# A decoder trunk whose FFN up projections become 2x2x2 block products in seven steps

## The chip, the cores and the metric

The kernel runs on one core of a Trainium2 chip. The metric is the device time of one execution in microseconds; the median of several runs counts.

## The reference, cut to what matters

Two layers work on a residual stream x of 1024 tokens and 1024 channels. Each ends in a convolutional FFN, with D_FF = 2816 and a causal convolution of width 3 over the tokens:

```python
def conv_ffn(h, w_up, w_dw, b_dw, w_down):
    u = h @ w_up                       # [1024, 1024] @ [1024, 5632]
    u = causal_dwconv(u, w_dw, b_dw)
    gate, val = jnp.split(u, 2, axis=-1)
    return (jax.nn.silu(gate) * val) @ w_down

x = x + conv_ffn(rmsnorm(x, g_ffn[l]), w_up[l], w_dw_f[l], b_dw_f[l], w_down[l])
```

Around it stand, in layer 0, a Conformer convolution module with a memory attention beside it and an output projection; in layer 1, a forgetting attention with a memory attention and an output projection. All is float32.

## The kernel before

Channels lie on partitions, tokens along the free axis, in two halves of 512 tokens (`HS`). x is eight tiles `x[k]` of 128 channels by 1024 tokens (tag `x`, eight buffers). A float32 operand is split in two parts that TensorE takes exactly: `split` (lines 77 to 85) makes hi on ScalarE by a cast (line 81) and lo = source - hi (line 82), on GpSimd where nothing else is named. `mm3` (line 103) then makes three matmuls for each k tile: hi hi, hi lo and lo hi.

`ffn` (line 336) first calls `normed` (line 174), which multiplies x by the gain of the norm and splits it (lines 168 and 169), and forms 1/rms of each token as a row `rb` on all partitions; the projection runs on the unscaled values and `rb` is multiplied into its result. `up(c)` handles the hidden tile c of 22: for the gate half and the value half (s = 0, 1) it loads a 1024 x 128 block of w_up, splits it, and makes for both token halves 8 k tiles x 3 matmuls of 512 columns, 96 in all, into a PSUM tile `u` of two banks. VectorE multiplies u by rb in PSUM (line 368), ScalarE applies the tap of the same token and the bias (Identity, line 371), VectorE adds the two earlier tokens from PSUM (lines 373 and 375), ScalarE applies Silu to the gate, VectorE multiplies gate and value (line 384), and the product g is split (tiles gh and gl). A block of w_down is loaded and split too.

Up and down alternate: with G = 2, after two new tiles c the down projection of the two tiles before is made. `down_part` (line 389) accumulates its tiles in one PSUM bank and VectorE adds that to x (line 393). In layer 1 the last two tiles go through `down_final`, 256 tokens at a time, with the last norm.

The order on each engine is worked out when the kernel is built, from the order in the text as priority and from modelled times. DMAs go through the queue of SyncE (SP). Raw weights have two buffers (`raw`), the split ones three (`wh`, `wl`), the w_down ones three of their own. PSUM has eight banks: `c0` to `c3`, used in a ring, and two pairs `b2a` and `b2b`.

Before the first FFN stands the output projection of layer 0 (`out_part`, line 328, called for both halves and m = 0 to 7), whose addition at line 334 finishes x[m].

Of the kernel before, what the change touches and what calls it, by code (L numbers as in the profile page):

```python
# [36 lines left out]
# columns of the packed per-channel vectors: name -> (number of columns)  # L37
# [14 lines left out]
class Trunk:  # L52
# [24 lines left out]
    def split(self, hi, lo, src, lo_eng=None, scale=None):  # L77
        """hi = float32r(src * scale); lo = src * scale - hi, both exact to 24 bits together."""
# [8 lines left out]
    def load_w(self, src, shape, gains=None, name="w", pools=None, lo_eng=None):  # L87
        """DMA one weight unit and split it; shape is the free shape of the unit."""
# [14 lines left out]
    def mm3(self, out, terms, start=True, stop=True):  # L103
        """out (+)= sum over terms of (ah + al)^T (bh + bl) without al^T bl (below 2^-24)."""
# [8 lines left out]
    # The projections run on x * gain; the factor 1/rms of a token is applied to their results  # L113
    # (in layer A to x before the split).
# [3 lines left out]
    def bcast_row(self, col, nb, tag="b1"):  # tag: of a new PSUM tile, or the place itself  # L118
        """col [128 tokens, nb] -> PSUM [128, nb*128] holding col as a row on every partition."""
# [7 lines left out]
    def rstd_cols(self, acc, nb, n, eps, ps=None):  # L127
        """acc [128 ch, nb*128 tokens] partial sums of squares -> 1/sqrt(mean + eps) [128 tokens, nb]."""
# [16 lines left out]
    def sum_squares(self, xs, w=HS, eng=None, tmp=None, two=None):  # L145
        """sum of the squares of xs; from index two on, a second sum on VectorE, added at the end."""
# [48 lines left out]
    def mem_k(self, mh, ml, rb, ks, wk):  # L195
        """K of the memory (stacked hi/hi and lo/lo), scaled."""
# [15 lines left out]
    def mem_v(self, mh, ml, rc, vs, wv):  # L212
        """V of the memory (hi | lo)."""
# [121 lines left out]

    def ffn(self, l):
        nc, tc = self.nc, self.tc
        with tc.tile_pool(name=f"ffn{l}", bufs=1) as fp:
            hh, hl, rb, _ = self.normed(f"f{l}", f"g_ffn{l}")
            gs = {}  # L340

# [968 lines left out]
```

## Time and profile before

| | |
|---|---|
| median of 3 runs | 2437.65 us (2437.09 to 2443.01) |
| span of the profiled execution, its first to its last instruction | 2435.7 us |
| whole time of the profiled execution | the profile gives only its span; the median of the runs is 1.95 us longer |
| TensorE busy | 2360.1 us, 97% |
| VectorE, ScalarE, GpSimd busy | 54%, 39%, 40% |
| mean granted TensorE clock | 0.988 |
| DMA | 156.93 MB, 64 GB/s in the mean |

The first FFN lasts from about 427 to 1146 us, the second from about 1692 us to the end. A row of a group of instructions gives the line of the kernel, the engine, the operation, output and inputs, and its count and durations. PE is TensorE, PEld its weight loads, DVE is VectorE, ACT is ScalarE, POOL is GpSimd and SP is SyncE. In a row of a stage stand its bounds and length, then for each engine the busy time and the count, then the granted clock, the busy share of the DMA engines and GB/s. In a row of the timeline stand start, length, engine, line and operation; `x2` means two of them in one row.

### The profile page before, as it was taken

What the parts mean: (1) busy time and instruction counts of PE and PEld (TensorE: products, weight loads), DVE (VectorE), ACT (ScalarE), POOL (GpSimd) and SP (SyncE); (2) the same over time, 40 slices, a digit from 0 to 9 for tenths busy, and PEclk for the clock granted to TensorE, in tenths of its full rate; (3) what the DMA queues carried; (4) which work ended last, traced back from release to release, by engine and by line L of the source; (5) the groups of instructions that cost most, each with busy time, mean ns of one, the idle gap of its engine ahead of it and who ended that gap; (6) DMA issues with size and microseconds to landing.
All of it is one profiled execution on the core that took longest, in us unless ns stands there. A gap on an engine that the chain in (4) does not pass through costs nothing.

```text
span 2435.7 us, 29247 instructions
## 1 busy us (share of the span) xinstructions
PE 2360.1 (97%) x11450; PEld 1964.7 (81%) x11450; DVE 1319.6 (54%) x1807; ACT 947.3 (39%) x1544; POOL 963.8 (40%) x643
## 2 busy tenths in 40 slices
PE   6999899999999999999998999999999999999998
PEld 6777678888888888887897888778888888888887
DVE  7489774444444444446646777854444444444436
ACT  6786655422222222223543665744322222222222
POOL 3686838422232323333423444525323222322223
PEclk9999989999999999999999999999999999999999
DMA  6110113211111111111432222331111111111112
GB/s 232 35 35 27 62 39 99 78 52 44 53 37 51 44 52 52 52 52 52 149 104 76 72 78 75 113 108 61 61 52 47 49 52 44 51 37 52 44 35 70
DMA packets 64537, 156.93 MB, mean 64 GB/s; under 512 B 6704, under 2 KB 26928, under 8 KB 64400
## 3 DMA queue, kind: packets, MB, share of 16 engines
q1 hardware_dynamic: 64256, 154.75, 20.4%
q8 instruction: 90, 1.47, 0.3%
q14 instruction: 47, 0.39, 0.0%
q10 hardware_dynamic: 144, 0.32, 0.0%
HBM read 128.63 MB, written 20.12 MB: 61 GB/s over the span
## 4 chain that ended last, share of the span: by engine, by line
PE 86%; DVE 6%; POOL 3%; ACT 2%; issue 2%; DMA 0%; DVEq 0%; POOLq 0%; ACTq 0%
PE u L108 13%; PE u L110 13%; PE u L109 13%; PE dn L108 6%; PE dn L110 6%; PE dn L109 6%; PE vps L850 3%; PE pq L108 2%; PE pq L110 2%; PE pq L109 2%; PE op L110 2%; PE op L109 2%; PE op L108 2%; PE fo L1033 1%; PE ft L1024 1%
## 5 line engine op out<-in xcount | busy, mean ns | idle before, releaser
L393 DVE TENSOR_TENSOR x<-x,dn 128x512 f32<-128x512 f32 (+1 forms) x368 | 241.1, 663 | 223.9 <-PE dn L110 221.0
L368 DVE TENSOR_TENSOR u<-u,rb 128x1024 f32<-128x1024 f32 x88 | 108.5, 1233 | 454.2 <-PE u L110 454.2
L82 POOL TENSOR_TENSOR wu_lo<-wu_raw,wu_hi 128x1024 fp32r<-128x1024 f32 x88 | 212.5, 2415 | 351.8 <-ACT wu_hi L81 351.8
L108 PE MATMUL dn<-gh,wd_hi 128*128 128x512 f32 (+1 forms) x736 | 282.1, 383 | 2.7 <-DVE x L393 2.5
L110 PE MATMUL dn<-gh,wd_lo 128*128 128x512 f32 (+1 forms) x736 | 279.7, 381 | 0.3 <-POOL wd_lo L82 0.3
L109 PE MATMUL dn<-gl,wd_hi 128*128 128x512 f32 (+1 forms) x736 | 279.9, 380 | 0.0
L108 PE MATMUL u<-f1h,wu_hi 128*128 128x512 f32 x704 | 274.5, 390 | 0.0
L108 PE MATMUL u<-f0h,wu_hi 128*128 128x512 f32 x704 | 274.5, 390 | 0.0
L109 PE MATMUL u<-f0l,wu_hi 128*128 128x512 f32 x704 | 274.4, 390 | 0.0
L110 PE MATMUL u<-f1h,wu_lo 128*128 128x512 f32 x704 | 274.3, 390 | 0.0
L109 PE MATMUL u<-f1l,wu_hi 128*128 128x512 f32 x704 | 274.3, 390 | 0.0
L110 PE MATMUL u<-f0h,wu_lo 128*128 128x512 f32 x704 | 274.2, 390 | 0.0
L82 POOL TENSOR_TENSOR wd_lo<-wd_raw,wd_hi 128x1024 fp32r<-128x1024 f32 x44 | 107.0, 2432 | 416.0 <-ACT wd_hi L81 416.0
L81 ACT CAST wd_hi<-wd_raw 128x1024 fp32r<-128x1024 f32 x44 | 46.2, 1050 | 449.2 <-PE dn L109 329.6
L82 POOL TENSOR_TENSOR gl<-y,gh 128x512 fp32r<-128x512 f32 x88 | 111.7, 1291 | 208.0 <-ACT gh L81 208.0
L81 ACT CAST wu_hi<-wu_raw 128x1024 fp32r<-128x1024 f32 x88 | 92.4, 1050 | 250.9 <-PE u L109 233.5
L373 DVE SCALAR_TENSOR_TENSOR y<-u,vecs,y 128x1023 f32<-128x1023 f32 x88 | 112.9, 1283 | 110.8 <-ACT y L371 110.8
L108 PEld LDWEIGHTS dn<-gh,wd_hi 128*128 128x128 f32 x736 | 138.3, 188 | 32.2 <-DVE x L393 5.0
L110 PEld LDWEIGHTS dn<-gh,wd_lo 128*128 128x128 f32 x736 | 138.1, 188 | 28.4 <-POOL wd_lo L82 0.5
L109 PEld LDWEIGHTS dn<-gl,wd_hi 128*128 128x128 f32 x736 | 138.5, 188 | 27.4
L108 PEld LDWEIGHTS u<-f1h,wu_hi 128*128 128x128 f32 x704 | 132.1, 188 | 28.0 <-issue 0.3
L108 PEld LDWEIGHTS u<-f0h,wu_hi 128*128 128x128 f32 x704 | 132.1, 188 | 28.0 <-issue 0.3
(349 smaller groups left out, 5399.3 us busy)
## 6 DMA issues: line engine op xcount, KB each, us to landing
wu_raw<-in_wup SPq DMA_DIRECT2D x88, 512.0 KB
wd_raw<-in_wdn SPq DMA_DIRECT2D x44, 512.0 KB
wia_raw<-in_wia SPq DMA_DIRECT2D x14, 512.0 KB
wo_raw<-in_wout SPq DMA_DIRECT2D x16, 384.0 KB
d_v<-vo SPq DMA_DIRECT2D x24, 256.0 KB
vsf<-d_v SPq DMA_DIRECT2D x12, 512.0 KB
x<-in_xT SPq DMA_DIRECT2D x16, 256.0 KB
x<-in_xT SPq DMA_DIRECT2D x8, 512.0 KB
```

The lines of the kernel that those rows point to most:

```text
L81: nc.scalar.copy(hi, src)
L82: (lo_eng or nc.gpsimd).tensor_tensor(lo, src, hi.bitcast(F32), op=ALU.subtract)
L108: nc.tensor.matmul(out, lhsT=ah, rhs=bh, start=start and i == 0, stop=False)
L109: nc.tensor.matmul(out, lhsT=ah, rhs=bl, start=False, stop=False)
L110: nc.tensor.matmul(out, lhsT=al, rhs=bh, start=False, stop=stop and i == n - 1)
L368: nc.vector.tensor_tensor(u, u, rb, op=ALU.mult)
L373: nc.vector.scalar_tensor_tensor(y[:, 1:], u[:, :S - 1], self.vec(wd, FW * j + 1), y[:, 1:], op0=ALU.mult, op1=ALU.add)
L393: return nc.vector.tensor_tensor(self.x[m][:, sl], self.x[m][:, sl], ps, op=ALU.add)
L850: nc.tensor.matmul(ps, lhsT=a[hf][k][:, tsl], rhs=w[:, k % 4], start=k == 0 and j == 0, stop=k == KD - 1 and j == 2)
L1024: mm = nc.tensor.transpose(pt[:, u, P:], p1[:, j * P:(j + 1) * P], self.ident)
L1033: nc.tensor.matmul(po, lhsT=vs[:, j], rhs=pl[:, u], start=False, stop=j == 2 * I + 1)
```

## The change

The two blocks of w_up of one c and the two halves of the input channels form a 2x2 block matrix A: A11 and A12 are the gate's rows for k tiles 0 to 3 and 4 to 7, A21 and A22 those of the value. B has the two halves of the channels (rows) by the two halves of the tokens (columns). Their product takes seven block products instead of eight (Winograd's form): of the left operands A11, A12, A22 and four sums S1 to S4, and of the right ones B11, B21, B22 and four sums T1 to T4.

- `ffn_operands` makes the right operands once for each FFN. x goes to DRAM (`d_x`) first, then its tiles are overwritten with the sums. T1 to T4 need both token halves.
- In `sums`, GpSimd makes S1 to S4 for each c, and `left` splits each of the seven left operands (128 x 512), two to a buffer of `wh` and `wl`; a fourth buffer is added.
- `p1` to `p7` are the products, 4 k tiles x 3 matmuls of 512 columns each, 84 for each c, in three PSUM banks. Between products that share a bank, ScalarE or VectorE reads the partial sum out; VectorE's additions combine them in SBUF tiles g and v (tag `x`). Product 4 of tile c comes after product 1 of tile c + 1.
- `conv` does what it did, but reads g and v in SBUF; the product goes to a DRAM tensor `d_g`.
- When all 22 tiles are done, x comes back from `d_x`, and the down projection runs over groups of 2, 4, 4, 4, 4 and 4 tiles; `prep` loads w_down and g and splits them, the low part of g on VectorE. The last four go through `down_final` in layer 1.
- The output projection of layer 0 takes m in the order 0, 4, 1, 5, 2, 6, 3, 7.

Comments and docstrings are dropped, which changes no instruction. The core of the diff, with the removed lines left out:

```diff
+    def chain(self, out, a, b, start):
+        nc = self.nc
+        ah, al = a
+        bh, bl = b
+        n = len(bh)
+        for k in range(n):
+            for j, (w, h) in enumerate(((ah, bh), (ah, bl), (al, bh))):
+                mm = nc.tensor.matmul(out, lhsT=w[:, k], rhs=h[k], start=start and k == 0 and j == 0,
+                                      stop=k == n - 1 and j == 2, skip_group_check=True)
+        return mm
+    def ffn_operands(self, l, fp):
+        nc = self.nc
+        K2 = KD // 2
+        gain = f"g_ffn{l}"
+        x = self.x
+        h0, h1 = slice(0, HS), slice(HS, S)
+        names = ("B11", "B21", "B22", "T1", "T2", "T3", "T4")
+        ops = {n: ([None] * K2, [None] * K2) for n in names}
+        def op(n, k):
+            for i in range(2):
+                if n in ("T1", "T2", "T3"):
+                    t = fp.tile([P, HS], F32R, tag="h2", name=f"f{n}{i}{k}", bufs=6 * K2)
+                else:
+                    t = self.htile(f"f{n}{i}{k}")
+                ops[n][i][k] = t
+            return ops[n][0][k], ops[n][1][k]
+        for k in range(KD):
+            for hf, sl in enumerate((h0, h1)):
+                nc.sync.dma_start(self.d_x[:, k, sl], x[k][:, sl])
+        for n, o in (("B11", 0), ("B21", K2)):
+            for k in range(K2):
+                self.split_gain(*op(n, k), x[k + o][:, h0], self.vec(gain, k + o))
+        rb = self.main.tile([P, S], F32, tag="rb", name="rb")
+        def stats(hf):
+            sl = (h0, h1)[hf]
+            acc = self.sum_squares([x[k][:, sl] for k in range(KD)], two=5 if hf else None)
+            def rest():
+                r = self.rstd_cols(acc, 4, D, self.eps_rms)
+                nc.scalar.copy(rb[:, sl], self.bcast_row(r, 4))
+            return rest
+        rests = [stats(0), stats(1)]
+        for k in range(K2):
+            g, g2 = self.vec(gain, k), self.vec(gain, k + K2)
+            x11, x12, x21, x22 = x[k][:, h0], x[k][:, h1], x[k + K2][:, h0], x[k + K2][:, h1]
+            nc.scalar.activation(x11, x11, AF.Copy, scale=g)
+            nc.vector.scalar_tensor_tensor(x12, x12, g, x11, op0=ALU.mult, op1=ALU.subtract)
+            self.split_gain(*op("B22", k), x22, g2)
+            nc.vector.scalar_tensor_tensor(x22, x22, g2, x12, op0=ALU.mult, op1=ALU.subtract)
+            self.split(*op("T2", k), x22, lo_eng=nc.vector)
+            self.split(*op("T1", k), x12)
+            nc.gpsimd.tensor_tensor(x11, x22, x11, op=ALU.subtract)
+            nc.vector.scalar_tensor_tensor(x21, x21, g2, x22, op0=ALU.mult, op1=ALU.subtract)
+            self.split(*op("T3", k), x11)
+            self.split(*op("T4", k), x21, lo_eng=nc.vector)
+        return ops, rb, rests
     def ffn(self, l):
         nc, tc = self.nc, self.tc
...
+        K2 = KD // 2
+        def unit(nm):
+            return self.main.tile([P, S], F32, tag="x", name=f"f{nm}")
+        with tc.tile_pool(name=f"up{l}", bufs=1) as fp:
+            no = [0]
+            def left(src):
+                i, j = divmod(no[0], 2)
+                no[0] += 1
+                if j == 0:
+                    if i % 4 < 3:
+                        w = [self.main.tile([P, KD, P], F32R, tag=t, name=f"f{t}") for t in ("wh", "wl")]
+                    else:
+                        w = [fp.tile([P, KD, P], F32R, tag=t, name=f"f{t}") for t in ("wh2", "wl2")]
+                    self.pair = w
+                hi, lo = (w[:, j * K2:(j + 1) * K2] for w in self.pair)
+                self.split(hi, lo, src)
+                return hi, lo
+            lo4, hi4 = slice(0, K2), slice(K2, KD)
+            raws = {}
+            def load(c):
+                if c >= NF or c in raws:
+                    return
+                a = self.main.tile([P, KD, P], F32, tag="raw", name="wa", bufs=self.NRAW)
+                b = fp.tile([P, KD, P], F32, tag="raw2", name="wb", bufs=2)
+                nc.sync.dma_start(a, self.wup[l, c])
+                nc.sync.dma_start(b, self.wup[l, c + NF])
+                raws[c] = a, b
+            st = {}
+            def sums(c):
+                a, b = raws[c]
+                s12 = unit("s12").rearrange("p (k c) -> p k c", k=KD)
+                s34 = unit("s34").rearrange("p (k c) -> p k c", k=KD)
+                g = nc.gpsimd
+                g.tensor_tensor(s12[:, lo4], b[:, lo4], b[:, hi4], op=ALU.add)
+                g.tensor_tensor(s12[:, hi4], s12[:, lo4], a[:, lo4], op=ALU.subtract)
+                g.tensor_tensor(s34[:, lo4], a[:, lo4], b[:, lo4], op=ALU.subtract)
+                g.tensor_tensor(s34[:, hi4], a[:, hi4], s12[:, hi4], op=ALU.subtract)
+                return {"S1": s12[:, lo4], "S2": s12[:, hi4], "S3": s34[:, lo4], "S4": s34[:, hi4],
+                        "A11": a[:, lo4], "A12": a[:, hi4], "A22": b[:, hi4]}
+            ops, rb, rests = self.ffn_operands(l, fp)
+            h0, h1 = slice(0, HS), slice(HS, S)
+            def p(c, n, a, b, bank, start):
+                d = st[c]
+                if start:
+                    tag = {"X": ("c0", "c1"), "Y": ("b2a", "b2b"), "V": ("c2", "c3")}[bank][c % 2]
+                    d[bank] = self.ps.tile([P, HS], F32, tag=tag, name="u" + bank)
+                self.chain(d[bank], left(d["A"][a]), ops[b], start)
+                return d, d[bank]
+            def p1(c):
+                load(c)
+                load(c + 1)
+                d = st[c] = {"A": sums(c)}
+                d["g"], d["v"] = unit("ug"), unit("uv")
+                d, X = p(c, 1, "A11", "B11", "X", True)
+                nc.scalar.copy(d["v"][:, h0], X)
+            def p6(c):
+                d, Y = p(c, 6, "S2", "T2", "Y", True)
+                nc.vector.tensor_tensor(d["g"][:, h1], Y, d["v"][:, h0], op=ALU.add)
+            def p5(c):
+                d, V = p(c, 5, "S1", "T1", "V", True)
+                nc.vector.tensor_tensor(d["v"][:, h1], V, d["v"][:, h0], op=ALU.add)
+            def p2(c):
+                d, X = p(c, 2, "A12", "B21", "X", False)
+                nc.scalar.copy(d["g"][:, h0], X)
+            def p7(c):
+                d, Y = p(c, 7, "S3", "T3", "Y", False)
+                nc.vector.tensor_tensor(d["v"][:, h1], Y, d["v"][:, h1], op=ALU.add)
+            def p3(c):
+                d, V = p(c, 3, "S4", "B22", "V", False)
+                nc.vector.tensor_tensor(d["g"][:, h1], V, d["g"][:, h1], op=ALU.add)
+                d["y"] = [conv(c, 0)]
+            def p4(c):
+                d, Y = p(c, 4, "A22", "T4", "Y", False)
+                nc.vector.tensor_tensor(d["v"][:, h0], Y, d["v"][:, h0], op=ALU.add)
+                y = conv(c, 1)
+                nc.vector.tensor_tensor(y, d["y"][0], y, op=ALU.mult)
+                nc.sync.dma_start(self.d_g[c], y)
+                del st[c]
+            def conv(c, s):
+                j = c + NF * s
+                u = st[c]["gv"[s]]
+                nc.vector.tensor_tensor(u, u, rb, op=ALU.mult)
+                y = unit("y")
+                wd = f"w_dwf{l}"
+                nc.scalar.activation(y, u, AF.Identity, bias=self.vec(f"b_dwf{l}", j), scale=self.vec(wd, FW * j + 2))
+                nc.vector.scalar_tensor_tensor(y[:, 1:], u[:, :S - 1], self.vec(wd, FW * j + 1), y[:, 1:],
+                                               op0=ALU.mult, op1=ALU.add)
+                nc.vector.scalar_tensor_tensor(y[:, 2:], u[:, :S - 2], self.vec(wd, FW * j), y[:, 2:],
+                                               op0=ALU.mult, op1=ALU.add)
+                if s == 0:
+                    nc.scalar.activation(y, y, AF.Silu)
+                return y
+            for c in range(NF):
+                p1(c)
+                if c == 0:
+                    p2(0)
+                    for r in rests:
+                        r()
+                else:
+                    p4(c - 1)
+                p6(c)
+                p5(c)
+                if c > 0:
+                    p2(c)
+                p7(c)
+                p3(c)
+            p4(NF - 1)
+        with tc.tile_pool(name=f"dn{l}", bufs=1) as fp:
+            self.ps.n = 0
             gs = {}
 
...
+            def prep(c):
+                w = self.load_w(self.wdn[l, c], [D], name=f"wd{l}",
+                                pools=None if c < 2 else ((fp, "dh", 7), (fp, "dl", 7)))
+                if c < 2:
+                    w = tuple(t for t in w)
+                g = self.main.tile([P, S], F32, tag="raw", name="g", bufs=self.NRAW)
+                nc.sync.dma_start(g, self.d_g[c])
+                hs = []
                 for hf in range(2):
...
+                    hi, lo = self.htile("gh"), self.htile("gl")
+                    self.split(hi, lo, g[:, hf * HS:(hf + 1) * HS], lo_eng=nc.vector)
+                    hs.append((hi, lo))
+                gs[c] = (hs, w)
+            def load_x(k):
+                self.x[k] = unit(f"x{k}")
+                nc.sync.dma_start(self.x[k], self.d_x[:, k])
+            def down_part(ts, m, hf, q=slice(0, HS)):
+                ps = self.ps.tile([P, HS], F32, tag="b1", name="dn")[:, :q.stop - q.start]
+                self.mm3(ps, [(wh[:, m * P:(m + 1) * P], wl[:, m * P:(m + 1) * P], hs[hf][0][:, q], hs[hf][1][:, q])
+                              for hs, (wh, wl) in ts])
+                sl = slice(hf * HS + q.start, hf * HS + q.stop)
                 return nc.vector.tensor_tensor(self.x[m][:, sl], self.x[m][:, sl], ps, op=ALU.add)
 
             def down(cs):
                 ts = [gs.pop(c) for c in cs]
                 for hf in range(2):
                     for m in range(KD):
...
+                        down_part(ts, m, hf)
 
...
+                        add = down_part(ts, m, i // 2, slice(i % 2 * Q, (i % 2 + 1) * Q))
...
+            G = 4
+            cs = [list(range(0, 2))] + [list(range(c, c + G)) for c in range(2, NF, G)]
+            for c in cs[0]:
+                prep(c)
+            for k in range(KD):
+                load_x(k)
+            for i, c in enumerate(cs):
+                for c2 in cs[i + 1] if i + 1 < len(cs) else ():
+                    prep(c2)
+                (down if l == 0 or i + 1 < len(cs) else down_final)(c)
...
-            for m in range(KD):
+            for m in (0, 4, 1, 5, 2, 6, 3, 7):
                 self.out_part(m, hf, self.load_wo(0, m, CT), mxh, mxl, range(CT))
...
+        self.d_g = dr.tile([NF, P, S], F32, name="d_g")
```

More of the change, by code (lines that the diff above doesn't have):

```diff
@@ L436, in down_final @@
                         scale(*q)
-            G = self.G
-            pend = None
-            for c in range(NF):
-                up(c)
-                if pend is not None and c % G == 0 and c < NF - G:
-                    down(pend)
-                    pend = None
-                if c % G == G - 1 or c == NF - 1:
-                    if pend is not None:
-                        down(pend)
-                    pend = list(range(c - c % G, c + 1))
-            (down if l == 0 else down_final)(pend)
+            G = 4
[8 more added lines that the diff above has]
+                (down if l == 0 or i + 1 < len(cs) else down_final)(c)
     def layer_a(self):
```

50 lines of the change are left out of this document (removed).

## The prediction

> **What bounds the kernel now.** I read the busy shares, then the chain that ended last, then the table by stage in the middle of the first FFN, then the groups of the two engines that the change loads.
>
> ```profile
> span 2435.7 us, 29247 instructions
> PE 2360.1 (97%) x11450; PEld 1964.7 (81%) x11450; DVE 1319.6 (54%) x1807; ACT 947.3 (39%) x1544; POOL 963.8 (40%) x643
> PE 86%; DVE 6%; POOL 3%; ACT 2%; issue 2%; DMA 0%; DVEq 0%; POOLq 0%; ACTq 0%
> ...
> 800.00:1000.00 200.00, 200.00 (x880) 164.83 (x880) 86.03 (x97) 47.23 (x49) 58.69 (x31) 1.00 0.15 48
> ```
>
> TensorE is busy all 200 us of that stage at a granted clock of 1.00, VectorE 86 us, GpSimd 59 us. So in the FFN matmuls set the time, one each 200 / 880 = 0.2273 us. (A matmul's own duration, 390 ns, overlaps the next one's and is no price.) A tile c has 96 up and 48 down matmuls, 144 x 0.2273 = 32.7 us, 21.82 us of it up.
>
> **What the products save.** Seven block products of 4 k tiles x 3 matmuls are 84 in place of 96: 12 fewer x 44 tiles x 0.2273 = 120 us. An up tile then needs 84 x 0.2273 = 19.1 us of TensorE. This is gained only if all that feeds TensorE fits in 19.1 us.
>
> **What feeds it.** These are the same operations in the trace of before, by shape (min/median/max ns):
>
> ```profile
> L82 POOL TENSOR_TENSOR gl<-y,gh x88: 1282/1291/1302, 462.7 to 2383.6; 128x512 fp32r<-128x512 f32 x88
> L82 DVE TENSOR_TENSOR wk_lo<-wk_raw,wk_hi x6: 1205/1214/2609, 1219.9 to 1446.9; 128x1024 fp32r<-128x1024 f32 x6
> L368 DVE TENSOR_TENSOR u<-u,rb x88: 1232/1233/1233, 446.8 to 2374.1; 128x1024 f32<-128x1024 f32 x88
> L375 DVE SCALAR_TENSOR_TENSOR y<-u,vecs,y x88: 1274/1282/1284, 450.6 to 2379.0; 128x1022 f32<-128x1022 f32 x88
> L169 DVE SCALAR_TENSOR_TENSOR f0l<-x,vecs,f0h x16: 739/1683/2769, 373.0 to 435.4; 128x512 fp32r<-128x512 f32 x16
> L393 DVE TENSOR_TENSOR x<-x,dn x368: 405/687/690, 497.3 to 2422.9; 128x512 f32<-128x512 f32 x168, 128x256 f32<-128x256 f32 x16
> L81 ACT CAST gh<-y x88: 620/622/629, 459.9 to 2382.2; 128x512 fp32r<-128x512 f32 x88
> L371 ACT ACTIVATE y<-u,vecs x88: 1187/1207/1212, 448.1 to 2375.4; 128x1024 f32<-128x1024 f32 x88
> ```
>
> Per up tile, GpSimd has 4 sums and 7 low parts of 128x512: 11 x 1.29 = 14.2 us. ScalarE has 7 casts and 2 copies of 0.62, 2 Identity of 1.21 and a Silu of about that: 9.2 us. VectorE has 5 PSUM additions (L393's 0.69), 2 multiplications by rb, 4 convolution steps and a last product of 1024: 5 x 0.69 + 3 x 1.21 + 4 x 1.28 = 12.2 us. Each alone fits. But look at the spread: L368, L375 and L393 read one operand from PSUM and never vary. L169 and wk_lo read both from SBUF and more than double at times. The change moves u from PSUM to SBUF (units g and v), so seven 1024-wide VectorE operations per tile go from the first kind to the second. What happens to that kind when GpSimd works:
>
> ```profile
> 423.53 2.40 POOL L82 TENSOR_TENSOR wu_lo<-wu_raw,wu_hi 128x1024 fp32r<-128x1024 f32 x1 [0.43 <-ACT wu_hi L81]
> 424.11 2.37 DVE L169 SCALAR_TENSOR_TENSOR f0l<-x,vecs,f0h 128x512 fp32r<-128x512 f32 x1 [0.80 <-ACT f0h L168]
> 425.89 1.72 POOL L157 TENSOR_TENSOR nsq<-nsq 128x512 f32<-128x512 f32 x1
> 428.68 4.00 DVE L169 SCALAR_TENSOR_TENSOR f0l<-x,vecs,f0h 128x512 fp32r<-128x512 f32 x2
> 430.39 1.74 POOL L157 TENSOR_TENSOR nsq<-nsq 128x512 f32<-128x512 f32 x1
> 480.83 2.53 POOL L82 TENSOR_TENSOR gl<-y,gh 128x512 fp32r<-128x512 f32 x2 [3.34 <-ACT gh L81]
> ```
>
> They take turns. GpSimd ends at 425.93 and the VectorE operation issued at 424.11 ends at 426.48, 0.55 later; the GpSimd addition issued at 425.89 ends at 427.61, 1.13 after that. Again at 430.39: the addition ends at 432.13, VectorE at 432.68. So a 128x512 GpSimd operation holds something for 1.13 us that a VectorE operation with two SBUF operands needs for 0.55 us per 512 columns. Per tile: 11 x 1.13 + 14 x 0.55 = 20.1 us, already over TensorE's 19.1.
>
> The Trainium skill (SBUF — State Buffer, "Who interferes with whom") names it: VectorE with two SBUF inputs contends with a GpSimd instruction that reads SBUF, and the loser blocks for the whole instruction. The trace agrees on who contends, but not on the length: a pair takes 1.13 + 0.55 = 1.68 us, not 1.29 + 0.74.
>
> **The pace I take.** The floor is 20.1 us a tile. GpSimd's own queue, in order, is 11 operations at the uncontended 2.53 / 2 = 1.265 us plus seven blocks of 1.10: 13.9 + 7.7 = 21.6 us. VectorE's loop through a tile bounds it from above: product 3, its addition (0.69), rb (1.13 + 1.10 = 2.23), Identity 1.21, two steps, product 4's addition, rb, Identity, two steps, last product, then product 5's addition, which comes after that one's chain and which the next product 3 waits for: 2.7 + 3 x 0.69 + 2 x 1.21 + 7 x 2.23 = 22.8 us. If nothing blocked it were 2.7 + 2.1 + 2.4 + 8.8 = 16.0, so TensorE's 19.1 is the other end. I take 21.6, since GpSimd then is never idle and meets each VectorE operation about once. Up tiles: 44 x (21.6 - 21.8) = -10 us (ends -120 and +44). Of the 120 us nearly all goes.
>
> **The front of each FFN.** Before, the splits run beside the output projection:
>
> ```profile
> 420.00:447.00 27.00, 27.00 (x136) 22.84 (x135) 12.97 (x11) 12.31 (x18) 16.90 (x8) 1.00 0.32 99
> 1690.00:1710.00 20.00, 18.89 (x96) 15.67 (x95) 13.46 (x11) 11.11 (x18) 15.79 (x9) 1.00 0.24 79
> L82 POOL TENSOR_TENSOR wo_lo<-wo_raw,wo_hi x24: 1812/1852/2397, 288.3 to 1659.7; 128x768 fp32r<-128x768 f32 x16, 128x1024 fp32r<-128x1024 f32 x8
> ```
>
> TensorE loses nothing at the first front and 1.1 us at the second. Now the operand sums add, per k, 6 VectorE operations (3.3 us of the shared resource) and 3 of GpSimd (3.4): 6.7, x 4 = 27 us. In layer 0 they come in the second half of the output projection, 8 x 18 x 0.2273 = 32.7 us, which holds 8 wo_lo (about 13.6) and some nine additions of squares (10); with sums(0) and three low parts (7.9) that is 58 us. TensorE has 32.7 + 5.5 (products 1 and 2): 20 late, less what only products 5 and 7 need (5): +15 us (0 to 20). In layer 1 only k = 2, 3 wait for the last two tiles of x: 13.4 + 5.6 + 7.9 = 27 us against 10.9 + 5.5; +10, less the 1.1: +9 (0 to 15). The reordered out_part only lets pairs k, k + 4 start earlier; its matmuls are the same. The 16 stores to d_x stand ahead of the w_up loads on SP, and x is overwritten only after them: 4.2 MB.
>
> **Up to down.** The pieces that must be there are x (8 loads), and w_down and g of the first groups through two raw buffers.
>
> ```profile
> 421.87 0.33 SPq L92 DMA_DIRECT2D wd_raw<-in_wdn  x1
> 425.63 1.05 ACT L81 CAST wd_hi<-wd_raw 128x1024 fp32r<-128x1024 f32 x1 [0.42 <-DMA wd_raw<-in_wdn]
> ...
> GB/s 0 0 0 0 0 0 0 0 0 0 0 0 0 413 413 118 413 321 0 0 0 360 413 387 406 406 406 400 413 413 400 216 347 236 243 210 256 308 426 419
> ```
>
> A load lands 3.8 us after issue; cast 1.05 and low part 2.4 make 7.2 us a raw buffer, g about 6, so four tiles take 4 x 13.2 / 2 = 26 us, while the first group (two tiles, 96 matmuls) covers 21.8. x and those four tiles are 8.4 MB, 20 us at 413 GB/s: DMA alone would fit. I take +5 for each FFN, +10 (0 if all is issued ahead; 30 if the last store, about 10 us of VectorE chain and 4 of landing, holds SP for both). In later groups 26 us stand beside 43.6 us of matmuls: nothing. The stores of g (0.5 MB a tile with 1 MB of weights in 21.6 us, 73 GB/s) are hidden behind the tile; without that cover each is 3.8 us. If x is late instead, L393's addition is what waits, and four PSUM banks behind it.
>
> **The end.**
>
> ```profile
> 2400.00:2408.00 8.00, 8.00 (x69) 1.00 0.00 0
> ```
>
> The last pass now holds four tiles: 384 matmuls of 256 columns at 8 / 69 = 0.116, not 192 plus 96 of 0.2273: 22.3 - 21.8 = +0.5 us. Half as many x additions are off the path: 0.
>
> **Sum.** -10 + 15 + 9 + 10 + 0.5 = +25 us on a span of 2435.7, so about 2461; the median of the runs is 2437.65, 1.95 over the span, so 2463 us.
>
> **The rivals.** (1) Faster: in the up loop the orders mesh, GpSimd runs during VectorE's five PSUM additions and its waits for ScalarE, and the pace comes near the floor of 20.1. That gives -75 + 35 = -40, 2398; with 20.5, 2415. It decides below 21.82 - 35 / 44 = 21.0 us a tile. For it: VectorE's additions (3.4 us a tile) read PSUM and do not block. Against: the loop above needs VectorE in a fixed order.
> (2) The blocking hardly matters, because the two engines meet seldom: TensorE keeps 19.1, -120 + 35: 2353. For it: L384 (before's last product) was never stretched. Against: there GpSimd worked 59 of 200 us, here 14 of 21.
> (3) VectorE's loop decides, 22.8 us: +44 + 35, 2515.
> (4) The blocking lasts the whole instruction: 11 x 1.29 + 3 x 1.21 + 4 x 1.28 = 22.9 us, +48 + 35, 2520. The trace's 1.68 us for a pair speaks against it. That is the rule of the Trainium skill's page SBUF — State Buffer.
> (5) Pace 21 and fronts as said: no change, 2437.
>
> **Chances.** Forecast (2440 to 2490) 0.48; (1) 0.25; (2) 0.06; (3) 0.07; (4) 0.04; (5) 0.10. Faster by over 0.3% (7 us, about what a measurement of this kernel can tell from none) 0.31, within 0.11, slower 0.58. The range leaves out (2), (4), part of (3) and the lowest of (1): 2390 to 2510. The forecast's own range is 2440 to 2490.
>
> **What would show it.** In the up stage of the changed kernel: TensorE busy under 95% with 84 matmuls per 21.6 us; GpSimd's 128x512 operations at a median near 1.7 to 2.3 us and VectorE's 1024-wide ones near 2.2, PSUM additions still 0.69. TensorE waiting for low parts of GpSimd or for VectorE's additions. 10 to 20 us idle at each front, some at the first down group. I am wrong if these durations stay at 1.29 and 1.28, or if TensorE is full all through the stage at 19.1 a tile.

## The result, and the profile after

The changed kernel takes 2536.57 us (median, 2535.83 to 2539.7), the kernel before 2437.84 us beside it: a ratio of 1.041 [1.039, 1.043], slower by 4.1%. Forecast were 2463 us, a range of its own from 2440 to 2490, and with the rivals 2390 to 2510: the sign is right, the size is not. The profiled execution has a span of 2537.9 us, 102 us more than before.

From the page of the changed kernel, the span, the busy shares, and the row on HBM:

```profile
span 2537.9 us, 29860 instructions
PE 2314.1 (91%) x11018; PEld 1885.6 (74%) x11018; DVE 1652.9 (65%) x1949; ACT 1087.9 (43%) x1884; POOL 1509.0 (59%) x969
...
HBM read 160.09 MB, written 51.58 MB: 83 GB/s over the span
```

TensorE lost 432 matmuls, and yet its share fell from 97% to 91%. DMA is not near a bound. The table by stage, in the middle of the first FFN's up projections:

```profile
490.00:930.00 440.00, 401.12 (x1662) 313.26 (x1662) 316.04 (x237) 163.54 (x237) 382.73 (x219) 0.98 0.22 70
```

TensorE is busy 401 of 440 us, and no engine is full: VectorE 316, ScalarE 164, GpSimd 383. What the prediction named as the test, min/median/max of the operations' durations in ns:

```profile
L82 POOL TENSOR_TENSOR fwl<-fs,fwh x176: 1257/2260/2300, 440.4 to 2249.4; 128x512 fp32r<-128x512 f32 x176
L516 DVE SCALAR_TENSOR_TENSOR fy<-fug,vecs,fy x44: 1272/2202/2219, 480.9 to 2266.5; 128x1022 f32<-128x1022 f32 x44
L496 DVE TENSOR_TENSOR fug<-uV,fug x44: 691/692/692, 473.9 to 2256.9; 128x512 f32<-128x512 f32 x44
```

GpSimd's low parts have a median of 2.26 us and VectorE's convolution steps one of 2.20, while the additions that read PSUM stay at 0.69. So the two engines do take turns. But the waits of the same stage name something else first (engine, line, what it waited for, us in total, times, longest):

```profile
ACT fy L513 <- DVE fug L510: 171.6, 20, 12.9
POOL fwl L82 <- ACT fwh L81: 57.3, 20, 6.4
DVE fug L496 <- PE uV L345: 38.0, 20, 2.7
ACT fwh L81 <- PE uY L345: 32.3, 9, 4.6
```

In each tile ScalarE stands 8.6 us in front of the Identity step of the convolution, which waits for VectorE's multiplication by rb; behind it in ScalarE's queue stand the casts of the next left operands. GpSimd then waits for a cast, 2.9 us a tile; these 57.3 us are all of its idle time in the stage (440 - 382.73). One case from the timeline: ScalarE stands from 491.96 to 501.92 us before an Identity, the casts behind it in its queue start at 503.53, and GpSimd, idle from 498.35, starts its low part at 504.23. The fourth row is the ring of left-operand buffers: a cast waits until TensorE has read the buffer's old contents. TensorE itself waits longest at product 4, which stands right behind product 7 on the same bank and needs VectorE's addition of product 7 first:

```profile
PE uY L345 <- DVE fuv L492: 12.2, 15, 0.9
```

Where the time went, from the ends of stages in the two traces, for the first and the second FFN, in us against TensorE's own time in the kernel before (21.8 an up tile; 240.0 for the 48 x 22 down matmuls). The first FFN of the kernel before ends at 1155 us, when its last down matmul ends, not at 1146:

| term | first | second | both, forecast | both, measured |
|---|---|---|---|---|
| front, to product 4 of the first tile | 49.6, not 21.8 | 50.3 | +24 | +56 |
| 20 tiles, mean pace | 22.52, not 21.82 | 22.45 | -10 (all 44) | +27 |
| last tile | 30.3 | 28.0 | | +15 |
| down stage | 249.6, not 240.0 | 255.5 | +10 | +25 |
| what the kernel before had lost itself | 8 | 10 | | -18 |

The last column adds up to +105; the 102 of the spans are left when some 2 us elsewhere are taken off. The last tile and the down stage belong together, since 24 matmuls of down (5.5 us) already run in the last tile.

### The profile page after: what moved, and what is told of

Same layout as the page of the kernel before. It is cut to its first block, busy times and chain, and to the rows that moved or that the text cites. A ratio compares the mean times of both kernels' runs of the same rounds, so it can differ in the third digit from the quotient of the medians.

```text
span 2537.9 us, 29860 instructions
## 1 busy us (share of the span) xinstructions
PE 2314.1 (91%) x11018; PEld 1885.6 (74%) x11018; DVE 1652.9 (65%) x1949; ACT 1087.9 (43%) x1884; POOL 1509.0 (59%) x969
## 4 chain that ended last, share of the span: by engine, by line
PE 32%; DVE 8%; POOL 5%; issue 3%; ACT 1%; DMA 1%; DVEq 0%; POOLq 0%; ACTq 0%; SPq 0%
PE uY L345 3%; PE dn L108 3%; PE dn L109 3%; PE dn L110 3%; POOL fwl L82 3%; PE vps L1020 3%; PE uV L345 2%; PE pq L108 2%; PE pq L110 2%; PE pq L109 2%; PE uX L345 2%; DVE fy L514 1%; DVE fy L516 1%; PE fs L1158 1%; PE fs L1159 1%
## 5 line engine op out<-in xcount | busy, mean ns | idle before, releaser
L345 PE MATMUL uY<-fT,fwh 128*128 128x512 f32 x1056 | 337.2, 400 | 44.0 <-DVE fuv L492 23.5
L82 POOL TENSOR_TENSOR fwl<-fs,fwh 128x512 fp32r<-128x512 f32 x176 | 336.6, 1926 | 66.5 <-ACT fwh L81 66.5
L108 PE MATMUL dn<-gh,wd_hi 128*128 128x512 f32 (+1 forms) x768 | 288.3, 378 | 27.1 <-DVE fx L565 22.8
L345 PEld LDWEIGHTS uY<-fT,fwh 128*128 128x128 f32 x1056 | 197.3, 190 | 102.8 <-DVE fuv L492 24.4
L345 PE MATMUL uX<-fB,fwh 128*128 128x512 f32 x704 | 231.1, 410 | 22.9 <-ACT fuv L476 22.6
L565 DVE TENSOR_TENSOR fx<-fx,dn 128x512 f32<-128x512 f32 (+1 forms) x208 | 131.3, 643 | 159.8 <-PE dn L110 157.5
L345 PE MATMUL uY<-fT,fwl 128*128 128x512 f32 x528 | 209.7, 397 | 7.6 <-POOL fwl L82 7.6
L345 PEld LDWEIGHTS uX<-fB,fwh 128*128 128x128 f32 x704 | 137.8, 197 | 57.7 <-ACT fuv L476 26.3
L82 POOL TENSOR_TENSOR fwl<-wa,fwh 128x512 fp32r<-128x512 f32 x88 | 144.2, 1640 | 52.5 <-ACT fwh L81 52.5
L345 PE MATMUL uX<-fB,fwl 128*128 128x512 f32 x352 | 144.0, 409 | 13.8 <-POOL fwl L82 13.8
L775 POOL TENSOR_TENSOR yp<-yp,ct 128x512 f32<-128x512 f32 x100 | 135.6, 1358 | 28.7 <-ACT ct L774 23.8
```

What stands on the lines that cost most here:

```text
L82: (lo_eng or nc.gpsimd).tensor_tensor(lo, src, hi.bitcast(F32), op=ALU.subtract)
L108: nc.tensor.matmul(out, lhsT=ah, rhs=bh, start=start and i == 0, stop=False)
L345: mm = nc.tensor.matmul(out, lhsT=w[:, k], rhs=h[k], start=start and k == 0 and j == 0, stop=k == n - 1 and j == 2, skip_group_check=True)
L565: return nc.vector.tensor_tensor(self.x[m][:, sl], self.x[m][:, sl], ps, op=ALU.add)
L775: nc.gpsimd.tensor_tensor(y[:, hf], y[:, hf], c, op=ALU.add)
```

## The experiments

The theory after the result (T1): the blocking costs most of the loss, and three other things have a part: ScalarE's order, the ring of left operands, and the fronts. The rival (T2): VectorE's and GpSimd's work alone sets the pace, and whatever is moved, TensorE waits the same.

### Without the blocking: e1_u_psum

```diff
-                nc.vector.tensor_tensor(u, u, rb, op=ALU.mult)
+                up = self.ps.tile([P, S], F32, tag="b2b", name="up")
+                nc.vector.tensor_tensor(up, u, rb, op=ALU.mult)
+                u = up
```

The sum of Y moves into halves of one PSUM pair to make room.

> Only the place changes where u times rb is written: a PSUM tile instead of the SBUF unit, so that Identity and the four convolution steps of a tile read u from PSUM; product Y's two banks become the halves of one PSUM pair to make room. Theory (VectorE with two SBUF operands and GpSimd exclude each other): three 1024-wide operations per tile still meet GpSimd instead of seven, 11 x 1.13 + 6 x 0.55 = 15.7 us a tile, under TensorE's 19.1; the convolution steps fall from 2.2 to 1.28 us, and the up pace from 22.5 to 19.1 to 19.8 us a tile: 2537 - 21 x 2 x 3 = about 2410 us (2395 to 2430). Rival (the pace comes from the order written out, the ring of left operands or the unit buffers): still 22 us or more a tile, 2520 to 2540 us.

Measured: 2474.26 us, 1.016 [1.015, 1.018] against before; 62 us of the loss are gone. The rows that answer to those above, and the stage:

```profile
L82 POOL TENSOR_TENSOR fwl<-fs,fwh x176: 1265/1302/2304, 440.6 to 2187.2; 128x512 fp32r<-128x512 f32 x176
L522 DVE SCALAR_TENSOR_TENSOR fy<-up,vecs,fy x88: 1273/1282/1286, 479.8 to 2213.5; 128x1022 f32<-128x1022 f32 x88
490.00:930.00 440.00, 409.31 (x1741) 323.68 (x1739) 283.06 (x256) 172.78 (x252) 322.23 (x223) 1.00 0.23 78
```

The same operations at 1.28 and 1.30 us: it was the second SBUF operand. TensorE's 308 products stand in the same order in both traces, so this comparison is clean on TensorE's side. The pace goes from 22.5 to 21.07 us a tile, not to TensorE's 19.1: 409 of 440 us. So the blocking is the largest cause that was measured, not the only one, and the time lies between the two forecasts. TensorE's longest wait is still the one at product 4, about half of all its idle time in the up stage (490 to 870 us):

```profile
PE uY L345 <- DVE fuv L496: 10.6, 13, 0.9
```

### The statistics at the front: e2_stats_later and e3_both

```diff
-                    for r in rests:
-                        r()
...
+                if c == 0:
+                    ring, self.ps.ring = self.ps.ring, ("c1", "c3")
+                    for r in rests:
+                        r()
+                    self.ps.ring = ring
```

The statistics' matmuls come after product 7 of the first tile instead of after product 2; e3 has this on e1.

> The matmuls of the norm's statistics (st and bc) are placed after product 7 of the first tile instead of after product 2; nothing else. Theory A: at the front TensorE stands behind these matmuls in its own queue, two gaps of 6 us per FFN, so 8 to 12 us per FFN go: about 2517 us. Theory B: the front waits for the operand sums T1 to T4 and the unit buffers that they free, and the gaps only move: within 6 us of 2537.

> The two edits together (u times rb to PSUM, statistics after product 7). If both theories hold the gains add: about 2390 us; if the front waits for the operand sums, the same as the first edit alone.

Measured: 2540.64 us (1.044 [1.042, 1.046]), and 2474.44 us for e3, like e1. The fronts stay at 50 us. TensorE's gaps of 6 us at these matmuls are no cause; without them it waits for operands.

### The ring, the order, the front on VectorE: e4 to e7

All four stand on e1.

```diff
+                no[0] = 8 * c                                    # e4: in p1
```
```diff
-                self.chain(d[bank], left(d["A"][a]), ops[b], start)
+                self.last_mm = self.chain(d[bank], left(d["A"][a]), ops[b], start)
...
+                with self.issue_after(self.last_mm.ins):         # e5: around product 4
```
```diff
-            self.split(*op("T1", k), x12)
-            nc.gpsimd.tensor_tensor(x11, x22, x11, op=ALU.subtract)
+            self.split(*op("T1", k), x12, lo_eng=nc.vector)
+            nc.vector.tensor_tensor(x11, x22, x11, op=ALU.subtract)
...
-            self.split(*op("T3", k), x11)
+            self.split(*op("T3", k), x11, lo_eng=nc.vector)      # e6
```

> On top of e1_u_psum, the ring of operand places starts anew at its first pair for every up tile (seven left operands, four pairs), so that no buffer phase runs through eight tiles. Theory A (what is left of the pace over 19.1 us is in part the ring: in three of every eight tiles a cast waits for a buffer that TensorE still reads, and TensorE then for the cast): the cycle 23.3, 22.9, 20.4, 20.4, 20.4, 20.4, 19.7, 23.0 vanishes, every tile takes about 20.4, the mean goes from 21.07 to 20.4, 40 x 0.65 = 26 us off 2474: about 2448. Theory B (the long tiles are long for another reason, such as the loads of weights): the cycle stays, 2474, or it is worse since the buffers come free no earlier.

> On top of e1_u_psum, product 4 of a tile is issued after product 1 of the next instead of right behind product 7, so that TensorE has a chain in another bank while VectorE adds product 7 into the sum of Y. Theory A (about 1.0 us of TensorE per tile is this wait for an addition of 0.69 us): the tiles of 20.4 become 19.5, 40 x 0.9 = 36 us off 2474: about 2438. Theory B (TensorE would only wait elsewhere, for the casts or low parts of the next tile, since VectorE and GpSimd are what sets the pace): 2465 to 2475.

> On top of e1_u_psum, in the operand sums of each FFN's front the low parts of two sums and one difference go from GpSimd to VectorE: per k VectorE has 9 operations and GpSimd none of these three. Theory A (at the front VectorE and GpSimd alternate without a gap, 1.7 us a pair, so a GpSimd step of 1.13 us is replaced by a VectorE step of 0.55): per k 3 x 0.58 = 1.7 us, 4 k and 2 FFNs: 14 us off 2474, about 2460; the front goes from 51 to about 44. Theory B (the front waits for one unit of x or one sum in a fixed order, not for the sum of the two engines' work): 2470 to 2478.

> On e1_u_psum all three: the ring anew for each tile, product 4 after product 1 of the next tile, and the front's three operations on VectorE. If each of the three causes is its own: -26 - 36 - 14 from 2474, about 2398, faster than the kernel before (2435). If the feeding engines set the pace whatever the order: 2440 to 2460, no faster than before.

Measured: e4 2521.36 us, e5 2473.17, e6 2468.06, e7 2514.80.

e4 is slower than e1 by 47 us. That is against theory A, and theory B had it only as "or it is worse"; but the edit settles the cause of the pattern: the eight-tile cycle vanishes, and every tile takes 22.0 us. With one half left unused, each tile has seven places instead of eight; this costs 0.9 us a tile, together with a change that the edit brings along: the builder now puts the products in one order in every tile, where e1 has an order that changes over eight tiles. In its up stage TensorE waits for casts once in each tile:

```profile
ACT fy L520 <- DVE up L516: 184.2, 39, 9.7
...
PEld uV L345 <- ACT fwh L81: 41.9, 20, 2.9
PE uV L345 <- ACT fwh L81: 33.5, 20, 2.5
```

This fits the view that TensorE lives on places that are ready early whenever ScalarE comes late.

e5 tells nothing: in e1 product 1 of the next tile already stands ahead of products 3 and 7, and product 4 right behind product 7 (in 42 of 44 tiles). The edit left the order of all 308 products as it was, and the wait for the addition with it. What that wait is worth was therefore not tested here. e6 takes 6 us off, 5 of them at the first front (46.7 for 51.7 us to product 4 of the first tile), none at the second. e7 inherits e4's loss.

### ScalarE's order: e8_identity, and alone e11_identity_alone

```diff
-            nc.scalar.activation(y, u, AF.Identity, bias=self.vec(f"b_dwf{l}", j), scale=self.vec(wd, FW * j + 2))
+            nc.vector.tensor_scalar(y, u, self.vec(wd, FW * j + 2), self.vec(f"b_dwf{l}", j), op0=ALU.mult, op1=ALU.add)
```

e8 has it on e1, e11 on the changed kernel as it is.

> On e1_u_psum, the two Identity steps of a tile (bias and first tap of the convolution) go from ScalarE to VectorE. Theory A (ScalarE works in order: in e1_u_psum it stands 165 us of 380 before an Identity that waits for VectorE, with the casts of the next products behind it, and GpSimd and TensorE behind these; this, not an engine's work, is what is left of the pace): TensorE no longer waits for casts, the pace goes from 21.07 to 19.5 to 20, 40 x 1.3 = 52 us off 2474, about 2422, faster than before's 2435. Theory B (the buffers of the left operands or VectorE's loop set it): VectorE has 2 x 1.28 us more per tile, the pace stays 21 or rises by up to 1, 2474 to 2510.

> The changed kernel with its unit in SBUF as it was, and only the two Identity steps on VectorE (one SBUF operand). Theory A (ScalarE's order is a cause of its own beside the blocking: there it stands 157 us of 400 before an Identity): about as much off as e8_identity takes off e1_u_psum. Theory B (with the blocking VectorE's and GpSimd's turns set the pace, 22.5 against my floor of 20.1, and ScalarE's wait is only their shadow): 2537 or up to 40 us more, since VectorE gets 2.5 us a tile in addition.

Measured: e8 2428.77 us, 0.997 [0.996, 0.998] against before: 45 us off e1, though VectorE got two operations of 1.34 us more in each tile. So the amount of VectorE's work was not what set e1's pace. Of e1's waits in the up stage this is the first:

```profile
ACT fy L519 <- DVE up L515: 185.4, 41, 11.4
```

It is gone in e8; what is left of that kind is ScalarE's wait before the Silu, 51.5 us from 490 to 860. But the edit did more than that: the builder made another order of the products. Product 4 stands right behind product 7 in 7 of 44 tiles only, and in 35 it has products of later tiles between, and TensorE's wait for the addition of product 7 falls to 5.6 us (490 to 860 us). The 45 us are those of ScalarE's freed queue and of the new order together; no run has one without the other.

But e11, the same edit with the blocking there, takes 2564.10 us, 27 more than the changed kernel. Its stage, and the new step:

```profile
490.00:930.00 440.00, 393.87 (x1607) 306.93 (x1605) 370.79 (x268) 117.86 (x192) 393.56 (x211) 0.96 0.20 69
L513 DVE TENSOR_SCALAR fy<-fug,vecs x44: 811/1666/2770, 474.9 to 2290.6; 128x1024 f32<-128x1024 f32 x44
```

GpSimd is busy 394 of 440 us and VectorE 371, and the pace is 23.6 us a tile: this fits theory B, that their turns are now the wall, though here too the order of the products changed. With the blocking, this move of work to VectorE costs; without it, the same move pays. So e11 fits T2, and e1 with e8 fits T1.

### Each place by itself: e9_places, and alone e14_places_alone

```diff
-                if j == 0:
+                if j == 0 and i < 4:
...
-                    self.pair = w
-                hi, lo = (w[:, j * K2:(j + 1) * K2] for w in self.pair)
+                    places.append(w)
+                hi, lo = (w[:, j * K2:(j + 1) * K2] for w in places[i % 4])
```

e9 has it on e8, e14 on the changed kernel.

> On e8_identity, the four pairs of left-operand buffers are allocated once per FFN, so that each of the 8 halves is waited for by itself and not with its neighbour. Theory A (a pair's two halves come free only with the later of two products; e4 showed that the ring's phase is worth 0.9 us a tile): the eight-tile cycle shrinks, 0.5 us a tile, 20 us off. Theory B (with ScalarE's queue free the casts no longer meet the ring): within 5 us of e8_identity.

> The changed kernel with only the places of e9 (8 halves, each waited for by itself), blocking and all else as it was. Theory A (the turns of VectorE and GpSimd set the pace, the ring only its pattern): pace 22 to 22.5, 2515 to 2540. Theory B (the ring is a cause of its own): the long tiles of 26 to 29 us go, pace 21.3, about 48 us off, 2490.

Measured: e9 2417.75 us, 0.993 [0.991, 0.994]; the pace goes from 20.5 to 19.7, and the stage is full:

```profile
490.00:860.00 370.00, 370.00 (x1602) 299.74 (x1601) 291.37 (x264) 119.97 (x189) 309.63 (x209) 1.00 0.23 79
```

TensorE is busy all 370 us, as in the kernel before, at 370 / 1602 = 0.231 us a matmul. The gain of seven products for eight is there at last: 19.7 for 21.8 us a tile. It is about half of what theory A forecast, and it cannot be put down to the places alone. The number of places is the same, and the order of the products changed once more: product 4 now stands behind product 2 or 5 of the next tile in 38 of 44 tiles, and no wait of TensorE is left in the stage. Counted from the starts of the matmuls in tiles 2 to 17, TensorE has 1.8 us a tile over 19.1 in e1, 1.1 in e8 and 0.3 in e9; of this 0.8, 0.6 and 0.0 are at product 4. So most of e9's gain over e8 came from where product 4 stands. (The ends of product 4 of successive tiles are now alternately 16.1 and 22.7 us apart; the pace is their mean.)

e14 is slower than both theories said: 2644.01 us, the slowest of all, 25.2 us a tile. Its waits in the up stage:

```profile
ACT fwh L81 <- PE uV L345: 140.2, 18, 9.9
POOL fwl L82 <- ACT fwh L81: 79.8, 18, 5.8
PEld uY L345 <- POOL fwl L82: 68.4, 18, 4.0
```

In each tile GpSimd now runs its eleven operations without a gap, most of them beside a VectorE operation and at 2.25 us (one such run lasts from 577.6 to 598.2 us in the trace), and then stands 4.4 us for a cast that waits for its place. The pace is a run of turns, 20.6 us, plus a wait in a fixed order, not the larger of the two. TensorE's granted clock in 490 to 930 us was 0.91, where e9's stage has 1.00, and that is in the pace too. The order of the products changed here as well: product 4 stands behind product 2 of the next tile in 38 of 44 tiles. Why the new places turn into that order was not taken apart.

### Product 3 after product 7: e10_all_four

```diff
+                with self.issue_after(self.last_mm.ins):
+                    d, V = p(c, 3, "S4", "B22", "V", False)
```

It also has e6's front.

> On e9_places, product 3 is issued after product 7 instead of before it (so that product 4 no longer stands right behind product 7 of the same PSUM bank and waits 1.0 us for an addition), and the front's three operations per k are on VectorE as in e6_front_vector. Theory A (TensorE's wait for the addition is then the last thing over 19.1): 40 x 0.9 + 6 = 40 us off e9_places. Theory B (the wait only moves): 0 to 6 us off.

Measured: 2587.35 us, 170 more than e9, against both theories. The wait of 1.0 us that was to go is one of e1's order; in e9 it had gone already. The edit puts products 7, 3 and 4 one behind the other in all tiles, so it takes product 4 back from behind the next tile's products. The pace is 23.7 us a tile, and the waits in the up stage begin with

```profile
ACT fwh L81 <- PE uV L345: 223.1, 33, 11.3
```

33 casts wait for 6.8 us each, for places that TensorE still reads. With product 3 later, its place comes free later; that this is the whole cause was not shown. The order of the products that the builder chose is part of how the places come round.

### What stayed open: e12_no_sums, e13_x_first

```diff
-            nc.vector.scalar_tensor_tensor(x12, x12, g, x11, op0=ALU.mult, op1=ALU.subtract)
...
-            nc.vector.scalar_tensor_tensor(x22, x22, g2, x12, op0=ALU.mult, op1=ALU.subtract)
...
-            nc.gpsimd.tensor_tensor(x11, x22, x11, op=ALU.subtract)
-            nc.vector.scalar_tensor_tensor(x21, x21, g2, x22, op0=ALU.mult, op1=ALU.subtract)
```
```diff
-            for k in range(KD):
-                load_x(k)
+            xl = [load_x(k) for k in range(KD)]
...
+                with self.issue_after(xl[3].ins if i == 0 else None):
+                    for c2 in cs[i + 1] if i + 1 < len(cs) else ():
+                        prep(c2)                                 # e13
```

> The changed kernel with the operand sums of the front left out (T1 to T4 are split from plain quadrants of x; five VectorE and GpSimd operations per k fewer, 20 per FFN; the output is not the reference's). Theory A (the front of 50 us is the queue of sums, 1.7 us a pair of turns): 20 operations, 12 to 20 us off each front, 2536 to about 2500. Theory B (the front is the splits, the squares and the statistics, which were there before, or waits for the first left operands): front 45 to 50 us, 2525 to 2537.

> On e9_places, the reload of x stands on SyncE's queue ahead of the loads of tiles 2 and 3 of the down stage, instead of behind them. Theory A (TensorE stands 9 us at the first down group of each FFN because x waits behind loads that wait for raw buffers): the gap falls to 0 to 3 us, 12 to 18 us off 2418, about 2403. Theory B (x waits for the last tile's own buffers, whatever the order): 2415 to 2420.

Measured: e12 2519.27 us, 1.034 [1.032, 1.035] (four operations per k fall away, sixteen per FFN, not the twenty of the expectation). Product 4 of the first tile ends 16.0 us sooner in the first FFN, at 460.6 for 476.6, and 9.7 us sooner after the start of layer 1 in the second; some 6 us are given back in the tiles. So the sums' arithmetic is 26 of the fronts' 56 us. What the other 30 wait for is not settled. The changed kernel's first front shows where TensorE loses them:

```profile
427.00:477.00 50.00, 31.73 (x124) 24.77 (x123) 38.10 (x31) 19.50 (x34) 36.13 (x24) 0.76 0.08 27
```

It is idle for 18 of 50 us, and its granted clock is 0.76, where the kernel before had 1.00: the 124 matmuls would be at most 28.2 us at 0.2273 each and take 31.7.

e13 takes 2418.20 us, 0.992 [0.990, 0.994], no different from e9. TensorE's longest wait for x fell, in e9 and then in e13:

```profile
PE dn L108 <- DVE fx L572: 9.2, 2, 8.9
```
```profile
PE dn L108 <- DVE fx L572: 5.3, 1, 5.3
```

and the time did not: from the end of the last up product to the end of down it is 248.8 us and 247.7 in e9. The trace of e13 shows where the gain went. At 934.7 us TensorE stands 3.1 us for a cast of g (the second down group), which e9 does not; the second FFN has 2.1 us of the same. The loads that were put behind x now come late, so the wait moved from x to g. In the first FFN these waits are 9.2 us in e9 and 8.4 in e13, and the granted clock beside the first of them is low (0.74 and 0.83 from 890 to 910 us): together this is most of what the down stage has over TensorE's own time.

### Together: e15_best

e13 with e6's front.

> e13_x_first with the front's three operations per k on VectorE (e6_front_vector). If both add to e9_places: 2418 - 15 - 6 = 2397, faster than before by 1.6%; if neither, 2418.

Measured: 2409.07 us (2404.73 to 2411.83), 0.988 [0.987, 0.990]. It is faster than the kernel before by 1.2% and than the changed one by 5.0%: the same seven products, with what feeds TensorE, and the order of the products, rearranged. The forecast of 2397 counted e13's gain, which did not come.

## Why the prediction was wrong

**The mechanism of the turns was right.** Durations of 2.26 and 2.20 us with PSUM additions at 0.69 are what "What would show it" asked for, and e1 shows the cause by taking it away: 62 of 99 us. But the forecast let the turns only eat up the gain, and its "slower" came from the fronts and the transition alone.

**"The pace I take" is the step that failed**: 21.6 forecast, 22.5 measured, +27 us for 40 tiles in place of -10 for 44. Its reason was that GpSimd is never idle. GpSimd is busy 382.73 / 440 x 22.5 = 19.6 us a tile, less than the 21.6, and idle 2.9, all of it waiting for casts of ScalarE. The prediction let each engine's sum bound the pace, and put ScalarE at 9.2 us of 19 with no further thought; it named the Identity only inside VectorE's loop. But in the trace the casts stand behind the Identity in ScalarE's queue and start only after its wait, 8.6 us a tile. How much of the pace this costs is argued from the waits and not shown: e8 takes the wait away and gains 45 us, but without the blocking and with another order of the products, and e11, with the blocking, is slower.

**TensorE's wait at product 4 had no term.** "What would show it" names waits for VectorE's additions, but the sum puts them at nothing. In the changed kernel and in e1 they are about 0.8 us a tile at product 4 (tiles 2 to 17, as above), and e9 got rid of them, e8 of a quarter, by the order that came out, not by intent.

**The ring was not in the prediction at all.** That `left` puts seven operands on eight places, two to a buffer, stood in front of it. It makes tiles of 19.4 to 29.5 us in a cycle of eight, which e4 shows by ending the cycle. What a place is worth is not shown by itself: 0.9 us a tile in e4 and 0.8 in e9 hold a change of the products' order each.

**"The front of each FFN" is the second mis-sized term**: +15 and +9 forecast with ends of 20 and 15, +28 and +28 measured, both beyond their ends. The price of the operations was not far off: of the 27 us of turns for each FFN, the four operations per k that e12 leaves out are (3 x 0.55 + 1.13) x 4 = 11, or 22 for both, and e12 gets back 26. What failed is the overlap: at the first front the forecast let 38 of 58 us of turns run beside the output projection and the first two products, and took 5 more as not needed yet. That left 15, and 28 were measured. The casts of T1 to T4 on ScalarE are in no term.

**"Up to down"** was +10 and is about +40 with the last tile. Moving the x loads forward, which the forecast thought of, only moves the wait to g (e13).

**The kernel before lost 18 us of its own** in the two FFNs, of which the forecast credited 1.1. This went the other way, and hid part of the error.

**The rivals.** (3) and (4) had the pace nearly right, 22.8 and 22.9. For (4) that is luck: GpSimd's 19.6 us a tile are below the 22.9 that whole-instruction blocking would fill, and a low part beside a VectorE step takes 2.26 us, not 1.29 + 1.28. (3) is not decided. e8 has no blocking and cannot speak to it; e11, with more work for VectorE and the blocking there, is slower, as (3) would have it. Against (3), TensorE waits only 6.1 of 440 us for product 5's addition, which closes its loop (490 to 930 us). (1) and (2) describe what can be had: e9 reaches 19.7, but only after three edits and with another order of the products. The range's upper end failed because all cases shared the same 35 us for fronts and transition, which were measured as 96.

## What to carry to other kernels

Summing each engine's work gives a floor; what decides is which instruction stands in front of which in an engine's queue, so read the waits of the half-empty engines too: a step that waits for another engine may belong behind, or off, the queue that feeds TensorE. When a change moves a VectorE operand from PSUM to SBUF while GpSimd works beside it, its price is the turns, and keeping one operand in PSUM takes them away. Buffers that rotate with another period than the loop make a cycle over several tiles; look at single tiles, not at the mean. Try fixes together, since here the same edit cost 27 us in one setting and gained 45 in the other. And where a builder works out the order, compare the order of the products before and after each edit: in e4, e8, e9, e10, e11 and e14 it moved, and the edit's own worth can't be told from that of the new order.

## What the runs showed of the hardware that was not expected

VectorE's step with a single SBUF operand also takes turns with GpSimd: in e11 the tensor_scalar of 128x1024 takes 0.81 us where no GpSimd operation overlaps (17 times, 0.815 at most) and 1.67 at the median where one does (71 times). From PSUM, in e9, it takes 1.34, though GpSimd works beside 87 of the 88:

```profile
L520 DVE TENSOR_SCALAR fy<-up,vecs x88: 1328/1343/1347, 476.4 to 2151.8; 128x1024 f32<-128x1024 f32 x88
```

The Trainium skill (SBUF — State Buffer, "Who interferes with whom") says that tensor_scalar can enter a two-port mode and then contends with GpSimd; the trace agrees, in the faster 0.81 and in the wait. For two-operand steps neither turn is a whole instruction: a low part and a convolution step, 1.28 us each when alone, take 2.26 and 2.20 when they alternate. That is near the 1.13 + 1.10 that the prediction had worked out, and less than 1.28 + 1.28.
